# A two-layer decoder trunk on one core: four small moves in the order of work and in who uses which buffer

## The chip, the core and the metric

One core of a Trainium2 chip. The engines are TensorE (PE, with its weight loads PEld), VectorE (DVE), ScalarE (ACT), GpSimd (POOL) and SyncE (SP), whose queue issues most of the transfers from HBM. The metric is device microseconds of one launch of the whole kernel.

## The reference, cut

Width 1024, 1024 tokens, two layers. `cond` is the SiLU of a conditioning vector; each layer takes six modulation vectors out of it.

```python
cond = jax.nn.silu(c)
for l in range(2):
    sh1, sc1, g1, sh2, sc2, g2 = split(cond @ ada_w[l] + ada_b[l], 6)
    h = rmsnorm(x, norm_g[l, 0]) * (1 + sc1) + sh1
    if l == 0:
        y = mlstm_mixer(h, ...)          # q, k, v, gates; chunkwise matrix memory, chunks of 128
    else:
        # shared latent: c_kv = rmsnorm(hk @ kv_w_a)[256], one rotary key of 64
        # k_nope, v = c_kv @ kv_w_b;  cq = rmsnorm(h @ w_q_a)[384];  q = cq @ w_q_b
        # causal softmax over 8 heads (128 plain + 64 rotary), then @ w_out
        y = mla_mixer(h, ..., k_nope, k_rope, v)
    x = x + g1 * rmsnorm(y, norm_g[l, 1])
    h = rmsnorm(x, norm_g[l, 2]) * (1 + sc2) + sh2
    y = square(relu(h @ w1[l])) @ w2[l]  # 1024 -> 4096 -> 1024
    x = x + g2 * rmsnorm(y, norm_g[l, 3])
```

Inputs and output are float32.

## The kernel before

All activations lie transposed (features on partitions, tokens along the free axis) in two halves of 512 tokens, `hfs[0]` and `hfs[1]`. A float32 product is made of three matmuls: each operand is split into a high part (a cast, on ScalarE) and a low part (the difference, on VectorE), and `mm3` (L278 to L282) multiplies high by high, high by low and low by high. Weights come in as tiles called `raw` and are split into `wh` (L238, ScalarE) and `wl` (L239, VectorE); `split_mod` does the same for activations (L499 and L500).

Buffers come out of rotating pools, each with a fixed number of tiles: `k4` 24, `hd` 8, `raw` 4, `ws` (the split weights) 8, `tmp` 3, `tmc` 6, `tma` 1, `v7` 1. In PSUM there are two banks `ps`, two banks `pc` and two double banks `pm`. Asking for a tile of a full pool means that the first instruction that writes it waits until the last reader of an older tile is done.

The program is written as Python generators which are woven together: each `yield` hands the turn to another stream. What is traced in this order is then scheduled, engine by engine, by a planner that simulates a timeline; every engine runs its own list in order, and SyncE its transfers too.

The stages in the order of time are: the first layer's projections, gates and mLSTM for both halves; its output projection; the first MLP, partly beside the second layer's latent projections and attention; the second MLP beside the attention of the second half; the output rows.

Four places matter here.

*Modulation.* `ada_chunk` (L372 to L396) makes 512 of the modulation's values: four quarters of the weight are loaded (L382) into `raw` tiles, VectorE multiplies them by `cond` and adds them up in the one `tma` tile (L388 for the first piece, L390 for the next seven), then TensorE turns the sum over and L366 and L367 finish it. `bgs` is the stream of these chunks; `with_bg(main, bgs, 1.5)` takes 1.5 steps of it for each step of `main`. Beside half 1's projections of q, k and v (`main`), `weave_n` runs `intra0(hfs[1])`, the mLSTM's scores: for each of four pairs of heads it asks for an `hd` tile and writes it with two multiplications (L792). The mixer's weights are loaded at L260, into `raw`.

*The MLP's steps.* A "hid" is 24 matmuls into a `ps` bank (one tile of hidden values, squared into an `hd` tile), an "up" is 24 matmuls into `pm`. In sweep 3 (half 1 of the first MLP, eight groups of two pairs) each hid needs two buffers from `pair_buf`: `tmc` and `tmp` in one turn, `v7` and `tmp` in the next, filled by the load L1079. L1088 and L1087 subtract and add, L984 and L985 square, L499 and L500 split. `steps` (L1220 to L1240) writes the list of hids and ups; with `own` the ups of a group stand right behind the group's own hids, without it they are spread among the next group's hids.

*The latent step* (L1601 to L1716). For each half it makes the shared latent (`hf.ckv`), the rotary key and the queries' latent (`hf.cq`). `behind()` sends off the values of a block: matmuls and two copies out of PSUM, at L499 and L500.

*The attention's keys and queries* (`kq` in `attention_first`): for each of eight heads it loads two weights, makes the keys and then the queries, each in a PSUM bank, and splits them (L499, L500).

The last two run as `other` in `two_streams`, the MLP's steps as `dense`. A number that `other` yields is a debt of dense steps: `due` grows by it, dense steps run while it is above zero, and an up or a hid takes 1 off (0.5 for each half of one). "align" runs dense steps until the next one is a hid.

```python
def two_streams(dense, other, fill=iter(()), more=3, rest=True):
    ...
        whole = n in ("align", "group")
        if not whole:
            due = due + n if n else 0
        while at not in ("lead", n == "align" and "hid") if whole else due > 0:
            was, at = at, go(dense)
    ...
            if not whole:
                due -= 0.5 if "within" in (was, at) else 1
```

Of the kernel before, what the change touches and what calls it, by code (L numbers as in the profile page):

```python
# [82 lines left out]
def kernel(  # L83
# [48 lines left out]
    def raw(dt=F32):  # L132
        return sb.tile([P, 1024], dt, tag="raw", bufs=RAW, name=f"raw_{next(uid)}")
# [233 lines left out]
        nc.vector.tensor_add(dst, s, bias)  # L367
        yield

    late, apart = [False], [False]  # L370

    def ada_chunk(w, c0, bias, dst):  # L372

        acc = tma()
        for q in range(4):
            if apart[0]:
                r = [tmc(), tmc()]
                for kk in range(2):
                    nc.sync.dma_start(r[kk], w[ts(2 * q + kk, P), c0 : c0 + 512])
            else:  # L380
                r = raw().rearrange("p (a b) -> p a b", b=512)
                nc.sync.dma_start(r, wcols(w, c0, 512, 2 * q, 2))  # L382
                r = [r[:, 0], r[:, 1]]
            for kk in range(2):
                k = 2 * q + kk
                with paced():
                    if k == 0:
                        nc.vector.tensor_scalar(acc, r[kk], cond[:, 0:1], None, ALU.mult)  # L388
                    else:
                        nc.vector.scalar_tensor_tensor(  # L390
                            acc, r[kk], cond[:, k : k + 1], acc, ALU.mult, ALU.add
                        )
            yield
        yield
        late[0] = True
        yield "wait"  # L396
        late[0] = False
        yield from ada_turn(acc, bias, dst)
# [569 lines left out]
    class Mlp:  # L968
# [248 lines left out]

            return prompt(load), out

        def steps(self, half, y, sweep, groups, prev=(), lead=False, own=False):  # L1220

            steps, prev = [], list(prev)
            for hids, fs in groups:
                done, n = 0, len(hids)
                for i, hid in enumerate(hids):
                    if lead:
                        steps += prev
                        done, lead = len(prev), False  # L1230
                    steps.append(hid)
                    while done * n < (i + 1) * len(prev):
                        steps.append(prev[done])
                        done += 1
                prev = [self.up(half, y, fs, j, sweep == 3 and fs[-1] == 2 * NPR - 1) for j in range(len(fs))]
                if own:
                    steps, prev = steps + prev, []
            return steps, prev

# [19 lines left out]
                p0 += n  # L1259
            return out  # L1260

        def sweep1(self, hf, y, sizes, own=False):
            g = self.groups(sizes, list, lambda p_: self.first(p_, hf.h2))
            return self.steps(0, y, 1, g, own=own)

# [17 lines left out]
            none = lambda: None  # L1283
            return steps + [(none, aside)] + last

        def sweep3(self, hf, y, sizes, buf, own=False):
            g = self.groups(
                sizes, lambda r: [*r, *(NPR + p_ for p_ in r)],
                lambda p_: self.third(p_, hf.ops, buf),
            )  # L1290
            steps, last = self.steps(1, y, 3, g, own=own)
            return steps + last
# [317 lines left out]
    def latent(hf, behind):  # L1610

        ready = []

        def load(b):
            with tc.high_priority(PRIO):
                w = []
                for i in range(1 if b == 2 else 2):
                    t = raw(F32R) if i else None  # L1620
                    if i == 0:
                        t = sb.tile([P, 1024], F32R, tag="ws", bufs=WS, name=f"lw_{next(uid)}")
                    nc.sync.dma_start(t.bitcast(F32), lw[b, i])
                    w.append(t.rearrange("p (a b) -> p a b", b=P))
                ready.append(w)

        load(0)
        load(1)
        yield 0
        h = hf.xn  # L1630

        def proj(b):
            if b < 4:
                load(b + 2)
            w, pt = ready.pop(0), pc() if b == 2 else ps()
            for k in range(KD):
                if b == 2:
                    nc.tensor.matmul(pt, w[0][:, k], h.lo[k], start=k == 0, stop=False)
                    nc.tensor.matmul(pt, w[0][:, k], h.hi[k], start=False, stop=k == KD - 1)
                else:  # L1640
                    mm3(pt, w[0][:, k], w[1][:, k], h.hi[k], h.lo[k], k == 0, k == KD - 1)
            return pt

        lb = lambda b: lbias[:, b : b + 1]
        hf.cs = hdv()
        for i in range(2):
            nc.sync.dma_start(hf.cs[:, i], rope_d[i][:, ts(hf.i, H)])
        if hf.i:
            hf.kk = [hd(F32R), hd(F32R)]
            for i in range(2):  # L1650
                nc.sync.dma_start(hf.kk[i][:, 0:H].bitcast(F32), kkd[i])
        else:
            t = hdv(F32R)
            hf.kk = [t[:, 0], t[:, 1]]
        s = ts(hf.i, H)
        ck, cq0, cq1 = k4v(), k4v(), k4v()
        cq = [cq0[:, 0], cq0[:, 1], cq1[:, 0]]
        def scaled(o, m):

            pt = proj(m)  # L1660
            if m < 2:

                evac(o, pt)
                pt = o

            if not rx:
                rx.append(sums_rstd(hf.xx, D, Cst.rearrange("p a b -> p (a b)")[:, :H]))
            nc.vector.tensor_mul(o, pt, rx[0])
            return o

        def based(o, m):
            nc.scalar.activation(o, scaled(o, m), AF.Identity, bias=lb(m))

        rx = []
        for m in range(2):
            based(ck[:, m], m)
        rp = rope_key(scaled(tmc(), 2), hf, lb(2))
        next(rp)
        yield 0
        rs = rstd_steps([ck[:, 0], ck[:, 1]], 256)  # L1680
        next(rs)
        based(cq[0], 3)
        yield 0
        kr = last_of(rp)
        rstd_k = last_of(rs)
        nc.scalar.copy(hf.kk[0][:, s], kr)
        nc.vector.tensor_sub(hf.kk[1][:, s], kr, hf.kk[0][:, s].bitcast(F32))
        if not hf.i:
            for i in range(2):
                nc.sync.dma_start(kkd[i], hf.kk[i].bitcast(F32))  # L1690
        for m in range(1, 3):
            based(cq[m], 3 + m)
        yield 0
        behind()
        rs = rstd_steps(cq, 384)
        next(rs)
        hi, lo = k4v(F32R), k4v(F32R)
        with paced():
            for m in range(2):
                u = ck[:, m]  # L1700
                nc.vector.scalar_tensor_tensor(u, u, col(KVL + m, 1), rstd_k, ALU.mult, ALU.mult)
                split_mod(hi[:, m], lo[:, m], u, None)
        hf.ckv = ([hi[:, m] for m in range(2)], [lo[:, m] for m in range(2)])
        yield 2
        rstd = last_of(rs)
        yield 0
        ah, al, b = k4v(F32R), k4v(F32R), k4v(F32R)
        his, los = [ah[:, 0], ah[:, 1], b[:, 0]], [al[:, 0], al[:, 1], b[:, 1]]
        for m in range(3):
            u = cq[m]  # L1710
            nc.vector.scalar_tensor_tensor(u, u, col(QL + m, 1), rstd, ALU.mult, ALU.mult)
            split_mod(his[m], los[m], u, None)
        hf.cq = (his, los)
        if not hf.i:
            behind()
        yield 1  # L1716

    SCALE = float((128 + 64) ** -0.5)
    wkvb, wqb = kv_w_b, b_w_q_b[0]
# [330 lines left out]
    def attention_first(hf):  # L2050
# [4 lines left out]
        def kq(hh):  # L2055
            p_, r = hh // 2, hh % 2
            w = wload(
                [
                    (0, 0, wcols(wkvb, hh * 256, P, 0, 2)),
                    (2, 0, wcols(wqb, p_ * 384 + r * 192, P, 0, 3)),  # L2060
                ],
                P,
            )
            yield
            kt, q = k4v(F32R), k4v(F32R)
            for t, k0, n, of, alloc in ((kt, 0, 2, hf.ckv, ps), (q, 2, 3, hf.cq, ps)):
                pt = alloc()
                for k in range(n):
                    mm3(pt, w[0][:, k0 + k], w[1][:, k0 + k], of[0][k], of[1][k], k == 0, k == n - 1)
                split_mod(t[:, 0], t[:, 1], pt, None)  # L2070
            for i in range(2):
                nc.sync.dma_start(kd[hh, i, :, ts(hf.i, H)], kt[:, i].bitcast(F32))
            keys[hh] = (kt[:, 0], kt[:, 1]), q
# [550 lines left out]
    drain(split_o(hfs[0]))  # L2624
    for _ in range(2):
        next(main)
    drain(weave_n(with_bg(main, bgs, 1.5), intra0(hfs[1]), 0.95))
    drain(bg0)
    B0 = gate(1, NG(0, 1), adac(0, G1))
    A1 = gain(2, NG(0, 2), adac(0, SC2))  # L2630
# [251 lines left out]
    def pair_tile():  # L2882
# [1 line left out]
        return t[:, 0:512], t[:, 512:1024]  # L2884

    two_streams(
        ms[0].run(ms[0].sweep3(hfs[1], z1, [2] * 8, pair_buf, True)),
        mixer1(hfs[0], z0, attention_first), bg_rest(),
    )

# [51 lines left out]
```

## Time and profile before

| | |
|---|---|
| time, median of three runs | 2306.42 us (2304.87 to 2309.31) |
| the profiled execution's own time | 2306.31 us |
| its span | 2304.5 us |
| TensorE, matmuls / weight loads | 2270.1 us / 1903.1 us, 11818 each |
| VectorE, ScalarE, GpSimd | 1691.3, 1125.9, 84.1 us |
| mean DMA rate over the span | 193 GB/s |

Busy time of matmuls is drawn with overlap: one of 512 columns is drawn about 0.39 us long, while the next starts 0.23 us later. In a row of the timeline the columns are start, duration, engine, line, operation, tiles (out<-in), shape and count; in square brackets stands how long the engine sat idle before it, and which engine's work on which tile and line ended that. Rows of the waits give the total, the number and the longest. SPq is SyncE's queue.

### The profile page before, as it was taken

How to read it: one execution, taken by the hardware profiler on the slowest of the kernel's cores; microseconds unless marked ns; L12 is line 12 of the kernel's file. 1: busy time of each engine (PE TensorE's matmuls, PEld its weight loads, DVE VectorE, ACT ScalarE, POOL GpSimd, SP SyncE). 2: the span in 40 equal slices, each digit the busy share in tenths (PEclk: the TensorE clock that was granted, in tenths of full speed). 3: DMA queues.
4: the chain of work that ended last, by engine and by line, in shares of the span. 5: the costliest groups of instructions: out<-in, count | busy, mean ns of one | idle time of the engine just before them, and what ended most of it. 6: DMA issues, size and time to landing. Idle time of an engine off the chain costs nothing.

```text
span 2304.5 us, 32036 instructions
## 1 busy us (share of the span) xinstructions
PE 2270.1 (99%) x11818; PEld 1903.1 (83%) x11818; DVE 1691.3 (73%) x2715; ACT 1125.9 (49%) x1915; POOL 84.1 (4%) x164
## 2 busy tenths in 40 slices
PE   8999999999999999999999999999999999999998
PEld 6888778888887878778888788888888888989997
DVE  6676776889887877677775687656666398798776
ACT  4354434765434445545444555434445354655453
POOL 1000000000122210000000000000000000000000
PEclk9999999999999999999999999999999999999999
DMA  9543464668999887566786655774434352545432
GB/s 322 180 125 118 131 182 149 195 217 267 332 281 299 285 281 284 187 204 210 233 254 195 226 195 154 250 233 158 139 97 155 103 166 83 159 139 180 123 110 110
DMA packets 399596, 444.33 MB, mean 193 GB/s; under 512 B 27123, under 2 KB 285232, under 8 KB 399440
## 3 DMA queue, kind: packets, MB, share of 16 engines
q1 hardware_dynamic: 386496, 397.09, 54.7%
q0 software_dynamic: 12944, 45.20, 5.2%
q8 instruction: 93, 1.52, 0.3%
q14 instruction: 63, 0.52, 0.1%
HBM read 343.65 MB, written 98.57 MB: 192 GB/s over the span
## 4 chain that ended last, share of the span: by engine, by line
PE 79%; DMA 8%; DVE 7%; issue 3%; ACT 2%; SPq 0%; POOL 0%; DVEq 0%; ACTq 0%; POOLq 0%
PE ps L280 13%; PE ps L281 13%; PE ps L282 13%; PE pm L281 9%; PE pm L280 8%; PE pm L282 8%; DMA raw<-in_mlp_w_dram 4%; PE pc L281 2%; PE pc L282 2%; PE pc L280 2%; DVE wl L239 1%; DVE k L247 1%; PE pc L1992 1%; PE pm L1792 1%; PE pm L1786 1%
## 5 line engine op out<-in xcount | busy, mean ns | idle before, releaser
L238 ACT CAST wh<-raw 128x1024 fp32r<-128x1024 f32 (+2 forms) x317 | 321.3, 1016 | 413.5 <-PE ps L281 173.3
L239 DVE TENSOR_TENSOR wl<-raw,wh 128x1024 fp32r<-128x1024 f32 (+2 forms) x317 | 375.2, 1185 | 192.5 <-ACT wh L238 173.8
L280 PE MATMUL ps<-k,wh 128*128 128x512 f32 (+1 forms) x1261 | 478.9, 380 | 5.7 <-DVE k L500 1.7
L282 PE MATMUL ps<-k,wl 128*128 128x512 f32 (+1 forms) x1261 | 471.8, 374 | 0.5 <-DVE wl L239 0.5
L281 PE MATMUL ps<-k,wh 128*128 128x512 f32 (+1 forms) x1261 | 471.2, 374 | 0.0
L280 PEld LDWEIGHTS ps<-k,wh 128*128 128x128 f32 x1261 | 237.6, 188 | 52.9 <-DVE k L500 3.0
L282 PEld LDWEIGHTS ps<-k,wl 128*128 128x128 f32 x1261 | 237.5, 188 | 43.8 <-DVE wl L239 1.2
L281 PEld LDWEIGHTS ps<-k,wh 128*128 128x128 f32 x1261 | 237.7, 189 | 41.5 <-issue 1.4
L247 DVE TENSOR_TENSOR k<-k,pm 128x512 f32<-128x512 f32 (+1 forms) x250 | 192.5, 802 | 63.7 <-PE pm L282 63.0
L280 PE MATMUL pm<-wh,hd 128*128 128x512 f32 x488 | 193.1, 396 | 1.6 <-DVE k L247 0.9
L282 PE MATMUL pm<-wh,hd 128*128 128x512 f32 x488 | 190.4, 390 | 0.0
L281 PE MATMUL pm<-wl,hd 128*128 128x512 f32 x488 | 190.4, 390 | 0.0
L280 PEld LDWEIGHTS pm<-wh,hd 128*128 128x128 f32 x488 | 91.7, 188 | 22.3 <-DVE k L247 2.0
L282 PEld LDWEIGHTS pm<-wh,hd 128*128 128x128 f32 x488 | 91.6, 188 | 19.9 <-DVE hd L500 0.5
L281 PEld LDWEIGHTS pm<-wl,hd 128*128 128x128 f32 x488 | 91.7, 188 | 18.4 <-issue 0.5
L280 PE MATMUL pm<-hd,wk 128*128 128x512 f32 x256 | 100.9, 394 | 1.6 <-ACT hd L499 1.6
L281 PE MATMUL pm<-hd,wk 128*128 128x512 f32 x256 | 100.1, 391 | 1.9 <-DVE hd L500 1.9
L390 DVE SCALAR_TENSOR_TENSOR tma<-raw,cond,tma 128x512 f32<-128x512 f32 x120 | 89.6, 747 | 16.5 <-DMA raw<-in_kv_ada_w_dram 8.1
L282 PE MATMUL pm<-hd,wl 128*128 128x512 f32 x256 | 99.8, 390 | 0.1
L280 PE MATMUL pm<-hd,wh 128*128 128x512 f32 x256 | 99.2, 390 | 0.6 <-ACT hd L499 0.6
L281 PE MATMUL pm<-hd,wh 128*128 128x512 f32 x256 | 99.6, 390 | 0.2 <-DVE hd L500 0.2
L282 PE MATMUL pm<-hd,wk 128*128 128x512 f32 x256 | 99.7, 390 | 0.0
(500 smaller groups left out, 4673.5 us busy)
## 6 DMA issues: line engine op xcount, KB each, us to landing
raw<-in_mlp_w_dram SPq DMA_DIRECT2D x176, 512.0 KB, 4.8
raw<-in_ada_w_dram SPq DMA_DIRECT2D x64, 512.0 KB, 4.7
raw<-in_mlp_w_dram SPq DMA_DIRECT2D x128, 256.0 KB, 4.9
raw<-in_a_w_in_dram SPq DMA_DIRECT2D x44, 512.0 KB, 4.1
lo<-wl POOLq DMA_DIRECT2D x32, 512.0 KB, 6.4
wk<-lo SPq DMA_DIRECT2D x64, 256.0 KB, 4.2
xs<-k SPq DMA_DIRECT2D x40, 256.0 KB, 3.9
raw<-in_a_w_out_dram SPq DMA_DIRECT2D x16, 512.0 KB, 5.4
```

The costliest lines, as they stand in the source:

```text
L238: nc.scalar.copy(hi[:, :n], r[:, :n])
L239: i = nc.vector.tensor_sub(lo[:, :n], r[:, :n], hi[:, :n].bitcast(F32))
L247: return f(*a, **k)
L280: nc.tensor.matmul(o, lh, rh, start=start, stop=False)
L281: nc.tensor.matmul(o, lh, rl, start=False, stop=False)
L282: pe_last[0] = nc.tensor.matmul(o, ll, rh, start=False, stop=stop)
L390: nc.vector.scalar_tensor_tensor(acc, r[kk], cond[:, k : k + 1], acc, ALU.mult, ALU.add)
L1786: nc.tensor.matmul(o[:, :w], ql, kh, start=True, stop=False)
L1792: nc.tensor.matmul(o[:, :w], qh, kh, start=False, stop=True)
L1992: nc.tensor.transpose(pt[:, ts(m, P)], u.prs[i][:, ts(kb, P)], ident)
```

## The change

1. `ada_chunk` can put a quarter of the modulation's weights into an `hd` tile instead of a `raw` tile (`spare`). That is switched on for the first eleven steps of the weave of half 1's projections with half 1's scores.
2. `own` is a number now: with 6, the ups of groups 0 to 5 of sweep 3 stand behind their own hids, as before, while group 6's ups are spread among group 7's hids and group 7's ups come at the end. Nothing else sets `own`.
3. In half 0's latent step `behind()` is called ahead of the three scalings and splits of the queries' latent, and the last yield is 1.5 instead of 1.
4. `kq` takes a `pc` bank for the queries instead of a `ps` bank.

```diff
-    late, apart = [False], [False]
+    late, apart, spare = [False], [False], [False]
...
     def ada_chunk(w, c0, bias, dst):
...
             else:
-                r = raw().rearrange("p (a b) -> p a b", b=512)
+                r = (hdv if spare[0] else raw)()
+                if not spare[0]:
+                    r = r.rearrange("p (a b) -> p a b", b=512)
                 nc.sync.dma_start(r, wcols(w, c0, 512, 2 * q, 2))
...
-        def steps(self, half, y, sweep, groups, prev=(), lead=False, own=False):
+        def steps(self, half, y, sweep, groups, prev=(), lead=False, own=0):
...
-            for hids, fs in groups:
+            for g, (hids, fs) in enumerate(groups):
...
-                if own:
+                if g < own:
                     steps, prev = steps + prev, []
...
         rstd = last_of(rs)
         yield 0
+        if not hf.i:
+            behind()
         ah, al, b = k4v(F32R), k4v(F32R), k4v(F32R)
...
         for m in range(3):
             u = cq[m]
             nc.vector.scalar_tensor_tensor(u, u, col(QL + m, 1), rstd, ALU.mult, ALU.mult)
             split_mod(his[m], los[m], u, None)
         hf.cq = (his, los)
-        if not hf.i:
-            behind()
-        yield 1
+        yield 1 if hf.i else 1.5
...
-            for t, k0, n, of, alloc in ((kt, 0, 2, hf.ckv, ps), (q, 2, 3, hf.cq, ps)):
+            for t, k0, n, of, alloc in ((kt, 0, 2, hf.ckv, ps), (q, 2, 3, hf.cq, pc)):
...
-    drain(weave_n(with_bg(main, bgs, 1.5), intra0(hfs[1]), 0.95))
+    spare[0] = True
+    for k, _ in enumerate(weave_n(with_bg(main, bgs, 1.5), intra0(hfs[1]), 0.95)):
+        spare[0] = k < 10
     drain(bg0)
...
-        ms[0].run(ms[0].sweep3(hfs[1], z1, [2] * 8, pair_buf, True)),
+        ms[0].run(ms[0].sweep3(hfs[1], z1, [2] * 8, pair_buf, 6)),
         mixer1(hfs[0], z0, attention_first), bg_rest(),
     )
```

More of the change, by code (lines that the diff above doesn't have):

```diff
@@ L1260, in groups, with sweep1 @@
             return out
-        def sweep1(self, hf, y, sizes, own=False):
+        def sweep1(self, hf, y, sizes, own=0):
             g = self.groups(sizes, list, lambda p_: self.first(p_, hf.h2))
@@ L1284, in sweep2, with sweep3 @@
             return steps + [(none, aside)] + last
-        def sweep3(self, hf, y, sizes, buf, own=False):
+        def sweep3(self, hf, y, sizes, buf, own=0):
             g = self.groups(
```

## Prediction

> **What bounds the kernel now.** I read the page's span and busy shares first, then the busy time by windows around the four places that the change edits, then the waits in those windows, and last the timelines of TensorE, VectorE and SyncE about each wait.
>
> ```profile
> span 2304.5 us, 32036 instructions
> PE 2270.1 (99%) x11818; PEld 1903.1 (83%) x11818; DVE 1691.3 (73%) x2715; ACT 1125.9 (49%) x1915; POOL 84.1 (4%) x164
> 225.00:285.00 60.00, 58.37 (x326) 46.97 (x324) 44.88 (x81) 22.71 (x41) 0.00 (x0) 1.00 0.49 145
> 940.00:975.00 35.00, 33.40 (x156) 26.92 (x155) 27.27 (x43) 21.76 (x35) 0.00 (x0) 1.00 0.68 205
> 975.00:1090.00 115.00, 110.67 (x590) 92.38 (x589) 89.63 (x166) 53.32 (x106) 0.00 (x0) 1.00 0.69 216
> 1265.00:1325.00 60.00, 57.27 (x247) 45.84 (x246) 40.07 (x57) 33.91 (x51) 0.39 (x4) 1.00 0.69 230
> ```
>
> TensorE is busy for 2270.1 of 2304.5 us: 34.4 us of idle time in all, and no edit here takes a matmul away. So the most that a reordering can win is some of those 34.4 us. In the windows' rows (length, then busy time of PE, PEld, DVE, ACT, POOL, then the granted clock) the idle time is 1.6, 1.6, 4.3 and 2.7 us, and the clock is 1.00 throughout. The question is which of these idle pieces the change reaches, and what comes in their place.
>
> How much does such a piece cost? Matmuls overlap, so the shown idle is not the whole loss.
>
> ```profile
> 955.84 0.39 PE L281 MATMUL ps<-k,wh 128*128 128x512 f32 x1
> 956.06 0.39 PE L282 MATMUL ps<-k,wl 128*128 128x512 f32 x1
> 957.83 0.50 PE L280 MATMUL ps<-k,wh 128*128 128x512 f32 x1 [1.38 <-DVE tmc L1088]
> ```
>
> Undisturbed, one 512-column matmul follows the other after 0.22 to 0.23 us, though each is drawn 0.39 us long. From 956.06 to 957.83 it is 1.77 us: 1.54 us lost where 1.38 is shown. I therefore add 0.16 us to every wait. [...]
>
> **Part d, modulation weights in hd.** Today they take turns in the four raw tiles with the weights that TensorE needs.
>
> ```profile
> SPq L260 <- DVE tma L390: 38.4, 10, 21.5
> 235.74 6.11 SPq L382 DMA_DIRECT2D raw<-in_ada_w_dram  x2
> 263.46 0.37 SPq L260 DMA_DIRECT2D raw<-in_a_w_in_dram  x1
> 262.17 0.48 DVE L388 TENSOR_SCALAR tma<-raw,cond 128x512 f32<-128x512 f32 x1
> ...
> 266.89 0.69 DVE L792 TENSOR_TENSOR hd<-pm,tmc 128x512 f32<-128x512 f32 x1
> 268.42 0.50 PE L280 MATMUL ps<-k,wh 128*128 128x512 f32 x1 [1.10 <-ACT wh L238]
> 269.68 0.50 PE L282 MATMUL ps<-k,wl 128*128 128x512 f32 x1 [0.53 <-DVE wl L239]
> 277.14 0.48 DVE L388 TENSOR_SCALAR tma<-raw,cond 128x512 f32<-128x512 f32 x1
> ```
>
> SyncE's queue stands from 241.9 (235.74 + 6.11) to 263.46: a mixer weight load (L260) waits 21.5 us for a raw tile that holds a quarter of modulation chunk 5. That quarter is not used up before 262.17, as the one tma accumulator is held by chunk 4. The load then comes late, and TensorE waits 1.10 and 0.53 us for its cast and its low part. The diff puts the quarters into hd while the first eleven steps of half 1's projections run, at 1.5 modulation steps each: 16 steps, which are chunks 4 and 5 and two quarters of chunk 6, ten loads. Then the raw tiles go to mixer weights alone, the load is issued some 20 us sooner, and both waits go: 1.10 + 0.53 + 2 × 0.16 = 1.95. Number and size of DMAs and of VectorE's multiplications do not change. Between 0 and 1.95 I take **1.9**, since 20 us of lead stand against 1.6 of wait.
>
> **Part a, values ahead of the queries' scalings.** In the latent step of half 0, the values' projection and its copies are now traced before the three scalings and splits of the queries' latent (L1711), and the step yields 1.5 in place of 1.
>
> ```profile
> 957.69 2.07 DVE L1711 SCALAR_TENSOR_TENSOR k<-k,cols,tmc 128x512 f32<-128x512 f32 x3
> 962.82 0.50 PE L281 MATMUL pc<-k,wh 128*128 128x512 f32 x1 [0.22 <-DVE k L500]
> 961.04 0.59 ACT L499 CAST k<-ps 128x512 fp32r<-128x512 f32 x1
> 963.29 0.68 DVE L500 TENSOR_TENSOR k<-ps,k 128x512 fp32r<-128x512 f32 x1
> ```
>
> At 957.83 (above) a ps bank is awaited, and VectorE's read of it (L1088) is late; the values' own copy out of ps ends only at 963.97 (963.29 + 0.68), queued behind 2.07 us of scalings and their splits. Ahead of them, the copies fall where TensorE fills the other bank, and both waits go: 1.38 + 0.22 + 2 × 0.16 = 1.9. What is late next: the queries' scalings, three multiplications and three splits by 0.68 us on VectorE, and whoever reads them (the rotary step, rot, and the first kq). For that the extra half yield puts one more "up" of the dense stream, 24 matmuls × 0.23 = 5.5 us, ahead of rot; it is taken off later, where the two streams align, so no work is added. But this up now follows its hid directly, and its first matmuls need that hid's squares; nearest rows are the waits of part c below, 0.34 to 1.34 us. Cost between 0 and 1.5, below nothing excluded since no wait is left to win; I take 0.6, so **1.3**.
>
> **Part b, q in pc.** Keys and queries of a head share the two ps banks with the dense hids; q now goes to pc.
>
> ```profile
> 1001.13 0.68 DVE L500 TENSOR_TENSOR k<-ps,k 128x512 fp32r<-128x512 f32 x1
> 1001.86 0.50 PE L280 MATMUL ps<-k,wh 128*128 128x512 f32 x1 [0.93 <-DVE k L500]
> 1080.54 0.50 PE L280 MATMUL ps<-k,wh 128*128 128x512 f32 x1 [0.72 <-DVE k L500]
> PE pc L1905 <- DVE sm L366: 0.7, 1, 0.7
> ```
>
> Twice a hid waits for a bank that kq's splits have not yet left: 0.93 + 0.72 + 2 × 0.16 = 2.0. With q in pc the hid finds a free ps bank. But pc's two banks serve the scores and the modulation's turns, and there one such collision costs 0.7 us already (last row). Eight heads can meet it none to two times, 0 to 1.7 us; I take 0.3, by six of eight heads that meet no wait now: **1.7**.
>
> **Part c, late last groups.** In sweep 3 the ups of a group so far follow its own four hids. Now only groups 0 to 5 do so; group 6's ups are spread among group 7's hids.
>
> ```profile
> 1282.83 0.49 PE L280 MATMUL pm<-hd,wk 128*128 128x512 f32 x1 [0.59 <-ACT hd L499]
> 1283.66 0.50 PE L281 MATMUL pm<-hd,wk 128*128 128x512 f32 x1 [0.34 <-DVE hd L500]
> ...
> 1282.92 0.69 DVE L500 TENSOR_TENSOR hd<-u,hd 128x512 fp32r<-128x512 f32 x1
> ...
> 1284.63 0.34 SPq L1079 DMA_DIRECT2D u<-u  x1
> ...
> u<-u SPq DMA_DIRECT2D x1, 256.0 KB, 5.4
> ...
> 1318.20 2.74 DVE L509 SCALAR_TENSOR_TENSOR k<-k,mods,tmc 128x512 f32<-128x512 f32 x4
> 1320.85 0.69 DVE L500 TENSOR_TENSOR hd<-tmc,hd 128x512 fp32r<-128x512 f32 x1
> 1321.60 0.50 PE L281 MATMUL pm<-hd,wk 128*128 128x512 f32 x1 [1.34 <-DVE hd L500]
> ```
>
> Three waits of ups for the squares of their last hid go: group 6's at 1282.83 and 1283.66 (0.59, 0.34), and group 7's at 1321.60 (1.34, where the mixer's four L509 stand ahead of the split L500): 2.27 + 3 × 0.16 = 2.75. Group 7's last ups do stay behind its last hid, so one wait may return there; its second hid is now followed by two ups of group 6 first, 2 × 5.5 us, for the others. What is added: hid 7's pair of buffers is asked for while group 6 still holds its own; all eight hd tiles are full for a while, and the load of u (L1079), which needs the single v7 buffer, takes 5.4 us to land. If hid 7's square stands on VectorE before it lands, what is queued behind it waits up to 1.1 us; if up 6's weights stand behind this load on SyncE's queue, TensorE waits up to 5.7 us (5.4 + 0.34). I take 0.7, nearer to the first: v7 is free when hid 6's split has read it at 1283.6 (1282.92 + 0.69), so the load lands about 1289, and the ps bank that its hid holds until then is not wanted again before two ups have run. **2.1**.
>
> **The sum.** 1.9 + 1.3 + 1.7 + 2.1 = 7.0 us. The profiled execution took 2306.31 us, 1.8 more than its span; the median of the runs is 2306.42, so both start points agree. 2306.3 − 7.0 = **2299.3 us**. About 0.2%, 4.6 us, is what a measurement of this kernel can tell from no change.
>
> **Rivals.** *One: the waits only move.* In parts a and c the copies and squares are not fewer, TensorE is 99% busy, and the next reader of a bank may stand just as late; then only d and b hold, 3.6 us, and a and c give −1 to 0 between them: 2303.4 (2306.3 − 3.6 + 0.7). For it speaks that each wait's releaser is VectorE, at 73% over the span but 78% (27.27 of 35) where part a lies; against it, that the order on VectorE itself changes. Chance 0.20.
>
> *Two, the slower side: the hd pool runs full in part d.* The scores' decay products take hd tiles too (L792 at 266.89 is the second of four pairs), beside the six quarters of chunks 5 and 6: six and two make eight, the whole pool. If one is asked for sooner than that sum allows, or the slots are handed round in order, L792 waits for the first use of chunk 6 (277.14, done 277.6), and VectorE's queue stands behind it, with the low parts (L239) of TensorE's weights in it: 277.6 − 266.9 = 10.7 us, or 8 if two weight tiles ahead still feed TensorE. Less the 5.1 of the other parts: 2309.2 to 2311.9. It decides when a ninth hd tile is asked for before 277. For it: the pool fits without a tile to spare. Against: chunk 4's quarters are used by then. Chance 0.14. [...]
>
> *Three: u's load holds SyncE's queue* and part c turns from 2.1 won to 3 to 3.6 lost: 2306.3 − 4.9 + 3.3 = 2304.7, chance 0.06.
>
> *Four: the change does not do what it says*, since the scheduler reorders by readiness and already puts these copies where they can go: 2304 to 2306, chance 0.06.
>
> **How the numbers follow.** The forecast has 0.54, with its own range 2295.5 to 2301.7. The low end is every added cost at nothing, 1.95 + 1.9 + 2.0 + 2.75 = 8.6 us, and 2.2 more, half of the idle time of the third window, for waits that go along. Rival one 0.20, two 0.14, three 0.06, four 0.06. Left out of 2295.5 to 2309.5 are some 0.07 below and the upper part of rival two. Faster by over 0.2% (below 2301.7): 0.54. Within 0.2%: one, three, four less 0.03 that they may fall beyond: 0.29. Slower: 0.14 + 0.03 = 0.17.
>
> **What would show it.** Part d right: no long wait of SyncE near 242 to 263, no wait of ps for wh near 268; wrong: L792 waits, and L239 after it. Part a right: nothing at ps for L1088, and none at the up after it. Part b: no ps wait for k in 975 to 1090, pc waits not above 1.5 us. Part c: TensorE's waits for hd near 1283 and 1321 gone, no longer wait than 0.5 about 1290. The forecast is wrong if TensorE's idle time falls by under 4 us, or if any new wait above 3 us stands in these windows.

## The result, and the profile after

| | before | changed |
|---|---|---|
| median | 2306.32 us (2304.87 to 2309.31, five runs) | 2296.14 us (2293.35 to 2297.86, five runs) |
| ratio | | 0.9948, 95% interval 0.9937 to 0.9959 |
| profiled execution / span | 2306.31 / 2304.5 us | 2293.35 / 2291.6 us |

The ratio makes 12.0 us (9.5 to 14.5); forecast were 7.1 below the median. A later comparison of the same two kernels gave a ratio of 0.9964 (0.995 to 0.9977), 8.3 us. Faster was right; the size was too small, and 2306.3 × 0.9948 = 2294.3 lies 1.2 us below the range's low end. The medians in the table lie only 10.2 us apart, and 2296.14 by itself lies inside the range, so by how much the range was missed depends on the measure. The two profiled executions lie 12.9 us apart.

First the changed kernel's page, then its busy time by the same four windows, moved to where the work now is:

```profile
span 2291.6 us, 32039 instructions
PE 2265.0 (99%) x11818; PEld 1904.4 (83%) x11818; DVE 1691.5 (74%) x2715; ACT 1126.3 (49%) x1915; POOL 84.3 (4%) x164
225.00:285.00 60.00, 60.00 (x349) 49.55 (x348) 46.95 (x83) 28.47 (x53) 0.00 (x0) 1.00 0.49 153
938.00:973.00 35.00, 34.31 (x160) 28.00 (x159) 25.99 (x40) 20.40 (x33) 0.00 (x0) 1.00 0.69 226
973.00:1088.00 115.00, 111.90 (x612) 94.61 (x611) 90.87 (x171) 56.52 (x114) 0.00 (x0) 1.00 0.66 208
1262.00:1322.00 60.00, 59.97 (x263) 49.02 (x262) 43.90 (x62) 36.06 (x56) 0.40 (x4) 1.00 0.75 249
```

TensorE's idle time fell from 34.4 to 26.6 us. In the first and the last window it is gone; in the middle two 0.7 and 3.1 us stay. The other 5.1 of the 12.9 us are busy time (2270.1 to 2265.0) of the same 11818 matmuls.

Where are the 12.9 us? The two traces hold the same number of working instructions on every engine, and outside four stretches every engine has them in the same order. So the start of the same matmul can be set against its start before. The table, worked out from the starts in each run's trace, gives the change of that difference over each stretch (positions in the trace of before, in us; minus is time won):

```
stretch (us)      3-220 220-331 331-700 700-760 760-932 932-990 990-1095 1095-1170 1170-1240 1240-1345 1345-2280
changed kernel    -0.59   -4.65    0.06   -1.13   -1.47   -1.09    -1.93      2.41     -0.15     -3.66     -0.81
e5 changed again  -0.51   -4.65   -0.32   -1.62   -0.38   -1.10    -3.09      3.77     -0.13     -3.62      0.27
e1 only d         -1.79   -4.65    0.08   -1.51   -0.89    0.01    -0.11      1.33     -0.13      0.18      0.15
e8 d, one chunk   -0.32   -3.67    0.25   -0.34   -0.18   -0.01     0.47     -0.19     -0.09      1.03     -0.47
e9 d to the end   -1.63   -0.16    2.57   -1.39   -0.62   -1.08    -2.85      5.15     -0.13      1.65      0.02
e2 only a         -1.23   -0.74   -0.59   -0.01   -1.09   -1.11     0.54     -0.17     -0.13      0.61     -1.24
e3 only b         -0.43    1.49   -0.33   -0.43   -1.40    0.00    -3.21      2.71      0.27      0.30     -1.23
e4 only c         -1.58   -0.50   -0.45    0.79    0.34   -0.01     0.02     -0.19     -0.13     -3.64     -1.15
e7 all but d       0.23    0.71   -0.25    0.15    1.22   -1.05    -0.47      2.09      1.03     -3.63      0.63
e10 all but b     -1.11   -4.65   -0.53   -1.74   -0.11   -1.08     0.23      0.87     -0.13     -3.65     -0.14
e11 c from 5      -1.75   -4.65   -0.57   -1.57   -2.14   -1.06    -1.42      4.22      0.01     -2.87      0.95
e6 b not head 6   -1.03   -4.65   -0.61   -0.63    0.60   -1.13    -2.38      0.08     -0.13     -3.65     -0.13
e12 the same       0.49   -4.65   -0.06   -1.35   -0.84   -1.06    -2.25      0.15      0.29     -3.63     -0.65
```

Two kinds of columns stand out. In some, every kernel with a part shows one number: -4.65 with all of d, -1.1 with a, -3.64 with c (e9, and for c e11, aside: their own edits change those stretches). In others the same order of work gives from -2.1 to +1.2 us with no edit near (760 to 932). A single pair of profiles can't be read in those. Of the 12.9 us, 2.9 lie in three columns without an edit (3 to 220, 760 to 932, 1345 to 2280).

A third kind of entry is a fall of TensorE's granted clock to 0.50, for 3.41 us. It makes e3 and e7 stand out from 220 to 331 (1.49 and 0.71; the clock falls at 269 and 270), e7 again from 990 to 1095 (-0.47; at 1021, behind an up's wait of 2.3 us) and e9 from 1095 to 1170 (at 1119, behind a wait of 2.64 us). The first column holds one such fall of before, between 28 and 60, by which its profile lost some 1.7 us (an estimate: 3.41 us at a clock of 0.50); of the other profiles only e12's has one there too. The windows' row of that stretch, before and then in e4:

```profile
28.00:60.00 32.00, 31.11 (x144) 23.81 (x143) 24.22 (x36) 12.04 (x18) 0.00 (x0) 0.95 0.87 309
```

```profile
28.00:60.00 32.00, 31.08 (x152) 24.17 (x150) 23.91 (x35) 12.25 (x18) 0.00 (x0) 1.00 0.87 307
```

**Part d** (4.65). SyncE's queue in the changed kernel:

```profile
250.65 3.12 SPq L384 DMA_DIRECT2D hd<-in_ada_w_dram  x4
258.14 8.02 SPq L260 DMA_DIRECT2D raw<-in_a_w_in_dram  x2
266.25 0.93 SPq L384 DMA_DIRECT2D hd<-in_ada_w_dram  x2
```

The stand from 242 to 263 is gone, and TensorE waits nowhere from 215 to 320. Before, a third wait stood behind the two that the prediction costs (the timelines of TensorE and VectorE before):

```profile
319.11 0.49 PE L830 MATMUL pm<-Cst,k 64*128 64x130 f32 x4 [1.33 <-DVE k L796]
...
316.63 1.23 DVE L239 TENSOR_TENSOR wl<-raw,wh 128x1024 fp32r<-128x1024 f32 x1 [1.22 <-ACT wh L238]
317.78 0.68 DVE L682 COPY k<-ps 128x512 f32<-128x512 f32 x1
318.38 0.68 DVE L796 TENSOR_TENSOR k<-k,pc 128x512 f32<-128x512 f32 x1
```

and the same work after:

```profile
313.88 0.49 PE L832 MATMUL pm<-Cst,k 64*128 64x130 f32 x4
...
310.59 1.23 DVE L239 TENSOR_TENSOR wl<-raw,wh 128x1024 fp32r<-128x1024 f32 x1 [0.79 <-ACT wh L238]
311.73 0.68 DVE L684 COPY k<-ps 128x512 f32<-128x512 f32 x1
312.33 0.68 DVE L798 TENSOR_TENSOR k<-k,pc 128x512 f32<-128x512 f32 x1
```

The state's update (L830, now L832) waits for a product (L796, now L798) that VectorE makes behind a weight split (L239), which itself waits for its cast. Before, the product was done at 319.06 and the update stood for it; now it is done at 313.01, 0.9 us ahead of the update. By starts the three waits cost 1.46, 0.70 and 1.54 us: 3.7 of the 4.65. The other 0.95 is spread in 0.1 to 0.3 us pieces at changes between streams.

**Part a** (1.1). The wait for a ps bank at 957.8 and the one at 962.8 (of a matmul into pc, for a value's low part) are gone, and the up right behind its hid waits:

```profile
955.96 0.50 PE L280 MATMUL pm<-hd,wk 128*128 128x512 f32 x1 [0.46 <-ACT hd L501]
956.68 0.50 PE L281 MATMUL pm<-hd,wk 128*128 128x512 f32 x1 [0.23 <-DVE hd L502]
```

**Part b.** Both waits of ps for k are gone, about 2.2 us (worked out under e10). A new one stands at 1127.5 (timelines of TensorE and VectorE after):

```profile
1123.88 0.60 PE L364 MATMUL pc<-ident,tma 128*128 128x128 f32 x4
...
1124.95 0.52 PE L1907 MATMUL pc<-ident,raw 128*128 128x128 f32 x3
1127.50 0.66 PE L1907 MATMUL pc<-ident,raw 128*128 128x128 f32 x4 [2.03 <-DVE sm L366]
...
1124.49 1.23 DVE L239 TENSOR_TENSOR wl<-raw,wh 128x1024 fp32r<-128x1024 f32 x1 [1.57 <-PE pc L364]
1125.63 1.21 DVE L247 TENSOR_TENSOR k<-k,pm 128x1024 f32<-128x1024 f32 x1
1126.76 0.68 DVE L366 TENSOR_REDUCE sm<-pc 128x4 f32<-128x512 f32 x1
```

The scores' turns (L1907) need two pc banks; one is held by a modulation chunk's turn (L364), whose reading (L366) stands on VectorE behind 2.4 us of other work. Before, this turn was put between the key's and the query's matmuls of head 6, 8.6 us ahead of the next scores. Now head 6's queries take that pc bank, and the turn comes after the following up, right ahead of the scores.

In some executions the wait costs more than itself. In e5, the same kernel, it is 1.91 us long, and the granted clock behind it is halved for 3.41 us:

```profile
1126.42 0.87 PE L1907 MATMUL pc<-ident,raw 128*128 128x128 f32 x4 [1.91 <-DVE sm L366]
...
1128.50:1130.00 1.50, 1.50 (x8) 1.41 (x8) 0.96 (x3) 0.00 (x0) 0.00 (x0) 0.50 0.40 101
```

That is why the column 1095 to 1170 has 2.1 to 2.7 us in three kernels with the wait, and 3.8 and 4.2 in two (e5, e11): about 1.6 us more where the clock falls.

**Part c** (3.65). The waits of the stretch are gone, the one at a ps bank near 1278 too. The load of u is out early:

```profile
1273.66 0.32 SPq L1081 DMA_DIRECT2D u<-u  x1
1275.40 0.90 SPq L1215 DMA_DIRECT2D raw<-in_mlp_w_dram  x2
1277.11 0.81 SPq L1216 DMA_DIRECT2D wk<-lo  x2
```

The next weights follow 1.7 us after it, in time: the fourth window is busy for 59.97 of 60 us.

### The profile page after: what moved, and what is told of

Its sections match the earlier page's. It is cut to its first block, busy times and chain, and to the rows that moved or that the text cites. A ratio compares the mean times of both kernels' runs of the same rounds, so it can differ in the third digit from the quotient of the medians.

```text
span 2291.6 us, 32039 instructions
## 1 busy us (share of the span) xinstructions
PE 2265.0 (99%) x11818; PEld 1904.4 (83%) x11818; DVE 1691.5 (74%) x2715; ACT 1126.3 (49%) x1915; POOL 84.3 (4%) x164
## 4 chain that ended last, share of the span: by engine, by line
PE 85%; DVE 5%; DMA 5%; issue 3%; ACT 2%; POOL 0%; SPq 0%; DVEq 0%; ACTq 0%; POOLq 0%
PE ps L280 14%; PE ps L281 13%; PE ps L282 13%; PE pm L281 10%; PE pm L280 10%; PE pm L282 9%; DMA raw<-in_mlp_w_dram 3%; PE pc L281 2%; PE pc L280 2%; PE pc L282 2%; PE pc L1994 1%; DVE k L247 1%; PE pm L1794 1%; DVE wl L239 1%; PE pm L1788 1%
## 5 line engine op out<-in xcount | busy, mean ns | idle before, releaser
L239 DVE TENSOR_TENSOR wl<-raw,wh 128x1024 fp32r<-128x1024 f32 (+2 forms) x317 | 375.3, 1186 | 196.2 <-ACT wh L238 175.8
L280 PE MATMUL ps<-k,wh 128*128 128x512 f32 (+1 forms) x1237 | 468.3, 379 | 0.3 <-ACT tmp L533 0.2
L282 PE MATMUL ps<-k,wl 128*128 128x512 f32 (+1 forms) x1237 | 462.1, 374 | 0.0
L281 PE MATMUL ps<-k,wh 128*128 128x512 f32 (+1 forms) x1237 | 461.7, 373 | 0.0
L280 PEld LDWEIGHTS ps<-k,wh 128*128 128x128 f32 x1237 | 233.1, 188 | 44.3 <-issue 3.0
L281 PEld LDWEIGHTS ps<-k,wh 128*128 128x128 f32 x1237 | 233.2, 188 | 40.6 <-issue 1.2
L282 PE MATMUL pc<-k,wl 128*128 128x256 f32 (+1 forms) x307 | 99.3, 323 | 0.5 <-DVE wl L239 0.5
```

The lines of the kernel that those rows point to most:

```text
L239: i = nc.vector.tensor_sub(lo[:, :n], r[:, :n], hi[:, :n].bitcast(F32))
L280: nc.tensor.matmul(o, lh, rh, start=start, stop=False)
L281: nc.tensor.matmul(o, lh, rl, start=False, stop=False)
L282: pe_last[0] = nc.tensor.matmul(o, ll, rh, start=False, stop=stop)
```

## The experiments

Each run is compared with the kernel before on its own chip; the table above has its stretches.

**One part alone: e1 (d), e2 (a), e3 (b), e4 (c).** Each is the changed kernel with the other three parts undone (of long lines, the words that change):

```diff
 # undo a
-        if not hf.i:
-            behind()
+        if False:
+            pass
...
-        hf.cq = (his, los)
-        yield 1 if hf.i else 1.5
+        hf.cq = (his, los); (behind() if not hf.i else None)
+        yield 1
 # undo b
-(q, 2, 3, hf.cq, pc)
+(q, 2, 3, hf.cq, ps)
 # undo c
-pair_buf, 6)
+pair_buf, 8)
 # undo d
-    spare[0] = True
+    spare[0] = False
...
-        spare[0] = k < 10
+        spare[0] = False
```

> Only part d (modulation weights in hd). Theory 1, the forecast's term: 1.9 us less than before, and the wait of pm at the state's update (L832, 1.3 us before, near 317) stays. Theory 2, read from the two traces: 4.7 us less by 340 us, the wait of pm near 317 gone too, and nothing more behind it. Theory 3: the 2.5 us that the changed kernel also won between 700 and 820 us, where every engine's order is the same as before, come from part d too: 7.2 us less in all, with the waits near 741 and 817 gone. Rival two of the forecast: slower, with L794 waiting.

> Only part a (values ahead of the queries' scalings, yield 1.5). Theory 1: 1.3 us less, 957.8's wait gone, 0.3 to 0.7 us of new waits of the up right behind it. Theory 2, that the 2.0 us wait for a pc bank behind L366 near 1127 comes with part a's shift of the streams and not with part b: 0.7 us more than before instead, with that wait in the profile.

> Only part b (the queries' bank from pc). Theory 1: the two ps waits for k near 1001 and 1080 gone, 1.7 us less. Theory 2: with them comes the 2.0 us wait for a pc bank behind L366 (2.2 us by starts), so 0.5 us more than before, which no measurement of this kernel tells from no change.

> Only part c (late last groups). Theory 1, the forecast's term: 2.1 us less. Theory 2, from the two traces: 3.7 us less, as all four waits of the stretch 1277 to 1322 go and none comes (0.46 us at a ps bank near 1278 among them). Rival three of the forecast: a wait of 3 us or more of up 6 for its weights near 1286, 1 to 2 us more than before.

| | ratio (95%) | us |
|---|---|---|
| e1, d | 0.9976 (0.9967 to 0.9984) | -5.5 |
| e2, a | 0.9999 (0.9991 to 1.0008) | -0.2 |
| e3, b | 1.0006 (0.9997 to 1.0015) | +1.4 |
| e4, c | 0.9983 (0.9974 to 0.9992) | -3.9 |

The forecast's terms for b and d fall, that for c lies at the interval's edge; that for a can't be told from nothing by its time. The four times add up to -8.2 us, beside -8.3 for all four together in e5 below. The stretches settle more: the readings of the first pair of traces return in the runs of single parts. The new wait belongs to b and not to a (waits of TensorE in e3 from 1090 to 1165):

```profile
PE pc L1907 <- DVE sm L366: 2.4, 1, 2.4
PE pc L1921 <- DVE k L502: 0.2, 1, 0.2
```

**e5, the changed kernel again.**

> The changed kernel again, for its time against the same before as the next three, and for a second profile. Theory 1, the four stages alone (4.65 + 0.6 + 0.5 + 3.65, read from the runs of single parts, between instructions whose order is the same): 9.4 us less than before, and the 2.6 us that the first profile also won between 700 and 830 us, where no engine's order differs, do not come back. Theory 2, that these belong to the change: 12 us less, with the same steps near 741 and 800 to 820.

2297.44 us (2293.24 to 2299.84), ratio 0.9964 (0.995 to 0.9977). The same stretches, and 1.6 us from 700 to 760 again.

**e6 and e12, head 6's queries in a ps bank.**

```diff
-(q, 2, 3, hf.cq, pc)
+(q, 2, 3, hf.cq, pc if hh != 6 else ps)
```

> The changed kernel, but the queries of head 6 take a ps bank as before. Theory 1: the 2.0 us wait of the scores' turns for the pc bank of the modulation's turn (L364, L366) comes from that turn finding both pc banks taken by head 6's queries, and being put behind the up; it goes, and the stretch from 1100 to 1165 is 2.0 to 2.3 us shorter than in the changed kernel: 11.5 us less than before. Theory 2: the turn would be late anyway, and another head's queries bring the wait back: no change against the changed kernel.

> The kernel with head 6's queries in a ps bank, once more, for its time beside the changed kernel's runs and a second profile. Theory 1: 2.2 to 2.75 us less than the changed kernel, 11 to 13 less than before, and no wait of the scores' turns over 1 us from 1100 to 1165. Theory 2, its first time was a lucky one: within 1 us of the changed kernel.

2291.81 us (2291.09 to 2298.22), ratio 0.9947 (0.9934 to 0.9959), and 2291.74 us (2288.2 to 2292.77), ratio 0.9941 (0.9928 to 0.9953). In e6's timeline of TensorE the turn is back at its old place and the scores' seven turns run in one go:

```profile
1117.27 0.60 PE L364 MATMUL pc<-ident,tma 128*128 128x128 f32 x4
1125.87 0.95 PE L1907 MATMUL pc<-ident,raw 128*128 128x128 f32 x7
```

The stretch 1095 to 1170 costs 0.1 us where it cost 2.1 to 4.2 in the five runs with all of part b (e9 aside); both waits for ps stay away. This kernel is 12.2 and 13.6 us ahead of before, the changed one 12.0 and 8.3. Its lead over the changed kernel, some 2.8 us between these means, is the size of the wait, but the intervals overlap; that it goes is shown by the traces.

**e7, all but d.**

> The changed kernel with modulation weights back in raw tiles. Theory 1, the parts add: 4.65 us more than the changed kernel, so about 4.8 less than before; the waits near 268 and 317 back (0.9 to 1.1, 0.5, 0.8 to 1.3). Theory 2, that the steps at 741 to 820 us are part d's doing: they are missing here and there in every profile with part d, so 7.2 us more than the changed kernel.

2304.72 us (2299.31 to 2307.93), ratio 0.9997 (0.9988 to 1.0006): 0.7 us less than before, where 4.8 were expected of the rest, and 7.3 more than e5. Theory 2 stands nearer, though the times of e2 to e4 add up to no more than -2.7, and the clock falls twice behind waits in this kernel's profile (near 270 and 1021); how much of the missing 4 us is such falls is open.

From 700 to 760 the eight profiles with all of d won 0.6 to 1.7 us (mean 1.4); the four without d lie between 0.4 won and 0.8 lost (mean 0.1 lost). Taken from 730 to 760 alone, seven of the eight, and e8 too, won 1.53, and e9 won 0.99; e3 won 0.68, and e2, e4 and e7 moved by less than 0.1. SyncE's queue there, from the same transfer on, before and then after:

```profile
725.05 0.37 SPq L1030 DMA_DIRECT2D raw<-in_mlp_w_dram  x1
725.84 2.08 SPq L260 DMA_DIRECT2D raw<-in_mlp_w_dram  x2
728.03 0.48 SPq L1030 DMA_DIRECT2D raw<-in_mlp_w_dram  x1
730.60 0.81 SPq L1035 DMA_DIRECT2D k<-m  x1
```

```profile
720.00 0.37 SPq L1032 DMA_DIRECT2D raw<-in_mlp_w_dram  x1
721.10 0.99 SPq L260 DMA_DIRECT2D raw<-in_mlp_w_dram  x2
722.49 0.37 SPq L1032 DMA_DIRECT2D raw<-in_mlp_w_dram  x1
728.37 0.34 SPq L1037 DMA_DIRECT2D k<-m  x1
```

The same transfers go out in the same order, but two of them trade their times. The load L1030 that goes out at 725.05 before (L1032 at 720.00 after) takes 7.8 us to land there and 5.9 here. A store that GpSimd issues just ahead of it (s<-k, at 724.66 and at 719.92) takes 5.9 us there and 8.4 here, and k<-m, which waits for that store, goes out 5.55 us behind the load there and 8.37 here. All nine profiles with a quarter of the modulation in hd, e8 and e9 among them, have the short load (5.8 to 6.0 us) and the long store (7.8 to 8.6); the other five have the long load (7.1 to 7.9) and the short store (5.9 to 6.0). So some 1.4 us go with part d, 380 us behind its last edit, in these profiles; why is open. It isn't the number of quarters moved: e8 moves four and the others ten.

**e8, one chunk in hd.**

```diff
-                r = (hdv if spare[0] else raw)()
-                if not spare[0]:
+                own5 = spare[0] and c0 == 8 * 512; r = (hdv if own5 else raw)()
+                if not own5:
```

with a, b and c undone.

> Before, with only the four quarters of the middle chunk (8 of the first layer's 12) in hd tiles, the one whose quarters hold the raw tiles while SyncE stands from 242 to 263; the chunks ahead and behind stay in raw tiles. Theory 1, the forecast's mechanism: this chunk alone holds up the mixer's weights, so the waits near 268 go here too, and 3 to 4.7 us come. Theory 2: the first and last chunk's quarters hold the raw tiles just as long, so SyncE's queue stands elsewhere and under 2 us come.

2301.17 us (2297.62 to 2302.9), ratio 0.9979 (0.997 to 0.9988). This chunk alone brings 3.67 of the 4.65 us; the two waits near 268 are gone, and what is left is

```profile
PE pm L832 <- DVE k L798: 0.5, 1, 0.5
```

So the forecast's mechanism for d is shown: the quarters of one chunk held the raw tiles.

**e9, quarters in hd to the end of the stretch.**

```diff
-        spare[0] = k < 10
+        spare[0] = k < 99
```

> The changed kernel with the modulation's quarters in hd tiles to the end of the stretch, not only for its first eleven steps. Theory 1, rival two of the forecast as a mechanism: with two quarters more per step the pool of eight runs full beside the scores' products, an L794 or a quarter's load waits for a tile, VectorE or SyncE stands behind it, and the stretch 225 to 331 us is 1 to 10 us longer than in the changed kernel. Theory 2: there is room, since quarters are used up in time: the stretch is as long as in the changed kernel within 0.3 us.

2308.3 us (2306.38 to 2313.6), ratio 1.002 (1.0011 to 1.0029): the whole gain lost, and more. In the stretch itself 4.5 us are lost against the changed kernel, in the range of theory 1, but not by its wait. No wait for an L794 stands in TensorE's list; the one wait from 215 to 345 is

```profile
PE pc L364 <- DVE tma L392: 2.1, 1, 2.1
```

a chunk's sum that comes late. The clock falls to 0.50 behind that wait, which is part of the 4.5 us. The larger loss is elsewhere, 2.5 us of it from 331 to 700 and 2.7 from 1095 to 1170. This is the only kernel whose order differs from the changed one's far from its edit (from 418 to 556, and at places from 970 to 1280): the planner came to other decisions there. From 1240 to 1345 it loses 5.3 us against the changed kernel, with

```profile
1252.20 0.50 PE L281 MATMUL pm<-hd,wk 128*128 128x512 f32 x1 [1.94 <-DVE hd L502]
1278.27 0.47 PE L280 MATMUL ps<-k,wh 128*128 128x512 f32 x1 [1.53 <-DVE u L1090]
1285.27 0.47 PE L280 MATMUL ps<-k,wh 128*128 128x512 f32 x1 [1.28 <-ACT tmp L986]
```

Whether that comes from the hd tiles' places in the rotation or from the planned times was not tried.

**e10, all but b.** Edit: undo b above.

> The changed kernel without part b (all queries in ps banks). Theory 1, part b won 2.2 us at the two ps waits and lost 2.75 at the modulation's turn: the waits near 990 (0.9 to 1.3) and 1070 (0.7) back, the one of 2 us near 1127 gone, and the time 0.5 us less than the changed kernel's, which a measurement can't tell. Theory 2, the forecast's term for b: 1.7 us more than the changed kernel.

2293.61 us (2292.81 to 2295.11), ratio 0.9954 (0.9941 to 0.9966), 10.6 us less than before. The ps waits are back, the one at 1127 is gone. Part b gains nothing that the times show: the five runs with all of it (e9 aside) won 2.0 us on average from 990 to 1095 and lost 3.0 to 1170; the four without it (e1, e2, e4, e10) lost 0.2 and 0.5. So 2.2 are won, 2.6 lost, and by these means it costs 0.4 us net, which is within the scatter of the columns (e7's fall of the clock stands in the 2.0).

**e11, late from group 5.**

```diff
-pair_buf, 6)
+pair_buf, 5)
```

> The changed kernel with own = 5: the ups of group 5 are spread among group 6's hids as well. Theory 1, what part c won were the waits of ups for their last hid's squares, and they stood only at groups 6 and 7, where the mixer's work is thick: nothing more comes, within 0.5 us in the stretch 1240 to 1345. Theory 2, spreading wins at every group: 0.5 to 1 us less again. Theory 3, rival three of the forecast: two more half-used hd tiles and a v7 load earlier, and a wait of over 1 us appears in group 5 or 6.

2295.54 us (2293.56 to 2298.17), ratio 0.9962 (0.9949 to 0.9974). The stretch wins 2.87 us instead of 3.64: 0.8 is lost again. That is more than theory 1's 0.5, and theory 2 falls. Theory 3 looked for a new wait of over 1 us; there is one of 0.9, and of another kind, a modulation turn (waits of TensorE from 1200 to 1340):

```profile
PE pc L364 <- DVE tma L392: 0.9, 1, 0.9
```

## Why the prediction was right or wrong

- **Faster, and by removed waits of TensorE:** right. Every wait that the four parts were said to remove is gone.
- **Part d, 1.9 us:** wrong, the step that failed. Its bound, "between 0 and 1.95", counted the two waits where the late weights are used and stopped there. The third wait, 50 us later at the state's update, is the same lateness handed on through VectorE's queue, and the 0.95 us of small pieces went with it. The runs show 4.65 in the stretch and about 1.4 more from 700 to 760. The mechanism, raw tiles held by one chunk, was right (e8).
- **Part a, 1.3 us:** right; 1.1, with 0.46 and 0.23 us of waits where 0.6 was set for them.
- **Part b, 1.7 us:** wrong. Its gain of 2.0 was right (2.2), its cost of 0.3 was not: one collision of 1.8 to 2.4 us, and at times the clock behind it, where "none to two times" 0.7 to 0.85 was allowed. The price was taken from a wait near 1062 in which VectorE's reading (L366) began 1.0 us after the turn was done; here it began 2.3 us after. The turn's new place, behind an up and beside a weight split, was not looked for, and the wait passed the prediction's own sign, pc waits not above 1.5 us.
- **Part c, 2.1 us:** too small. The 0.7 for v7 and SyncE's queue was nothing; the wait at 1277.86 (0.62 by starts), which the prediction did not name, went as well, and one wait cost 0.27 us beside its idle and not 0.16 (1283.66). 3.65.
- **The sum:** 6.05 + 1.1 - 0.4 + 3.65 = 10.4 from the stretches (d's 4.65 and 1.4 together), beside 12.0 and 8.3 measured. Two terms were too low by 5.7 together, one too high by 2.1. The low end of the range stood for 10.8 us, the parts' waits at no cost (8.6) and 2.2 for waits that go along. By the stretches' 10.4 the time would be 2295.9, just inside it, since b took back 2.1 of the 5.7 that d and c won beyond their terms. The 1.6 us that put the first comparison below the range are not found in any part, and the second comparison's 8.3 lies inside: on which side of the low end the time fell is in part luck, the sizes of d, b and c are not.
- **Rivals:** the waits only move: no for c, in part for a (1.67 won, 0.57 lost behind it), yes for b. The hd pool full: not in the changed kernel, where L794 holds up nobody; e9 goes over the edge, by another wait. u's load: no. The edit without effect: no.
- **Idle time as the room:** the prediction took what can be won from the 34.4 us of idle time, with 0.16 us added to each wait. Of the 12.9 us, 7.8 came out of idle time and 5.1 out of busy time at the same 11818 matmuls, while the weight loads' time moved by 1.3 us (1903.1 to 1904.4). Read from idle time alone, the gain would be 7.8 us.

## What to carry to other kernels

When a load is late, follow the lateness to the end of the stretch: here the split that it delayed stood in VectorE's queue, the product behind it came late too (the wait of 1.33 us at 319.11), and the gain was 4.65 us where the waits at the load's own readers cost 1.46 and 0.70. When a buffer user is moved to another pool, look for every user of that pool and ask where each will be put now; here one turn of 0.6 us went to the worst place, and leaving a single head as it was kept the gain without the cost (0.1 us from 1095 to 1170 in e6 and e12, 2.4 in the changed kernel's first profile). To tell 2 us of 2300, set the starts of the same instructions of two traces against each other, stretch by stretch, and use several executions to learn which stretches move by themselves.

## What was not expected of the hardware

TensorE's granted clock fell to 0.50 behind waits of about 2 us and less, and not behind all of them. In the fourteen profiles it fell twelve times ahead of the last 10 us, each time for 3.41 us. The waits of 1.91 (e5), 2.36 (e11), 2.3 (e7, at 1019) and 2.10 and 2.64 us (e9, at 314 and 1116) were followed by a fall; those of 2.03 (the changed kernel), 2.37 (e3), 2.00 (e8, at 1075) and 1.8 us (e7, at 1137) were not. The two waits near 268 (0.9 to 1.2 and 0.5 us) came before one in e3 and e7, and not in the profiles of before, e2 and e4. Where it fell, e9's 512-column matmuls followed one another after 0.43 us in place of 0.23, from 317.9 to 320.0. Between 28 and 60 even waits under 1 us came before a fall, in the profiles of before and of e12 (mean clock of that window 0.95 in both), in none of the other twelve (1.00); in the first 25 us it fell in three (the changed kernel, e3, e7). What sets it off is not shown. Behind the new wait of part b a fall cost about 1.6 us (the column 1095 to 1170). The prediction read the clock in its four windows alone, where it is 1.00 throughout; the same trace has a fall to 0.50 at 45.9.

The same work in the same order took different times in different executions, at a granted clock of 1.00: the stretch 760 to 932 ranges over 3.4 us (2.14 won in e11, 1.22 lost in e7). The stretch of part d, once no wait for a load was left in it, took the same time to 0.01 us in all seven profiles that have the whole of it.
